# Expert outputs combined through a one-hot matrix in fp32r, with the expert rows in two parts, the routing weights as scalars of the sum, the last stores issued by ACT, and one more load buffer

## The chip, the cores and the metric

The kernel runs on one core of a Trainium2 chip. The metric is the device time of one execution in microseconds, as the median of three runs. A profile of one more execution gives the span of the engines' work and every instruction in it. The engines are named PE (TensorE, matmuls), PEld (its weight loads), DVE (VectorE), ACT (ScalarE), POOL (GpSimd) and SP (SyncE, which here only issues DMAs).

## What is computed

A layer has two sub-layers on 256 tokens of 2048 channels, in float32. The first is a mixer (three token mixers, gated and projected); the change leaves its arithmetic alone. The second is a mixture of 16 SwiGLU experts, of which each token uses two. Cut to that:

```
h = rms_norm(x, g_norm_ffn) * (1 + scale_f) + shift_f
affinity = sigmoid(h @ w_router)                      # 16 experts
e_idx = the two best experts of the best group of four, by affinity + b_router
w_sel = affinity[e_idx] / sum(affinity[e_idx])
combine = sum(one_hot(e_idx) * w_sel)                 # tokens x 16
for e in range(16):
    act = silu(h @ w_gate[e]) * (h @ w_up[e])         # 2048 -> 1024
    y += combine[:, e:e+1] * (act @ w_down[e])        # 1024 -> 2048
x = x + gate_f * y
```

## The kernel before

**Two stretches.** Until about 853 us the mixer runs; its weights arrive in fp32, ACT casts each to a high part and DVE subtracts for a low part (type fp32r, `split_w`, L168 and L169; `split_to`, L173 and L174, does the same for other tiles), and PE multiplies three products per pair (L331 to L333). A short router stretch follows. From 869.58 us to the end the experts run, one after the other.

**One expert.** Each expert has 64 slots. `rank` (tokens x experts) says in which slot of an expert a token sits, and `cmb` its weight. A one-hot matrix `O` (tokens x slots, bf16, L1007) gathers the expert's tokens: matmuls of `h2`, the normed activations in three bf16 parts, with `O` (L1075). `Or` (L1015) and the matmuls at L1063 give each slot its token's scale `rB` (copied by ACT, L1065); DVE makes `X` of it (L1079, L1081), the expert's input with channels on the partitions. The weights of the expert come in 24 loads of 1 MiB (`load_e`, L853, all issued by SP): 8 for gate, 8 for up, 8 for down. Each load feeds one unit of four fp32 matmuls of 64 rows into a tile `ring` of PSUM (L1110; a unit leaves 8 records in the trace, since an fp32 matmul leaves two). There are three `ring` tiles. After a gate or up sum ACT copies the ring to `graw` (L1132, one buffer), PE transposes it (L1137), and ACT's SiLU (L1145) or DVE's product (L1151) makes `sgt` and `A`. The down weights give the expert's rows in two halves of 1024 channels; DVE multiplies each by the gate vector `gfB` into a tile `y` (L1163).

**The combine before.** `scatter` makes `OT` (slots x tokens, fp32): DVE builds a one-hot that already holds the weights (L1094), PE transposes it (L1095), ACT copies it (L1097). `combine_part` multiplies `OT` with 512 columns of `y` in fp32 (L1170) and DVE adds the result to `x2` (L1171); eight such parts make an expert.

**Order.** `up_unit`, `gate_unit` of the next expert and `down_unit` follow each other, and after each unit `between` takes one small job from the lists `soon` (gather and scatter of the next expert) and `todo` (combine parts). A scheduler then sets the order on each engine from its own estimates, so what stands where is read from the program, below. Each engine works through its own row in order.

**Load buffers.** Loads rotate through a stock of 1 MiB buffers: 17 when the experts begin (named `wr`, `ws` and `m` after their pools: 11 `wr`, 3 of the pool of the split weights, 3 of the four `m`), 14 from expert 0's down unit on, when one pool is given back. The fourth `m` buffer is used for `y` (`m_tile`), which takes one of the `m` in turn.

**The end.** The last expert's down weights come as four column blocks of two loads each. `give_out` combines one block, and SP stores each 128x512 piece of the result (L1223). Behind it stands a loop for experts with more tokens than slots (L1238 on), which this input does not enter.

Of the kernel before, what the change touches and what calls it, by code (L numbers as in the profile page):

```python
# [20 lines left out]
P = 128  # L21
# [32 lines left out]
def kernel(  # L54
# [707 lines left out]
    mH, mL = [[m_tile([P, KD // 2, S], F32R) for _ in range(2)] for _ in range(2)]  # L762
# [47 lines left out]
    r2 = constb.tile([P, NT], F32, name="r2c")  # L810
    shT = constb.tile([P, KD], F32)
# [50 lines left out]
    for n in range(4):  # L862
# [7 lines left out]
        for k0 in range(0, KD, 4):  # L870
# [15 lines left out]
            if n == 3 and k0 == KD - 4:  # L886
                rotate([wraw] * NRAW + [wrawb] * NRAWB + [wrawc] * NRAWC + [wraw2] * NRAW2 + [wspl] * 3 +
                       [mt_pool] * (NM - 1))
# [5 lines left out]
        def h2_first(t):  # L894

            vc = fn.tile([P, 512], F32, name="tmp", bufs=3) if n < 3 else vc3[:, t, :]
# [9 lines left out]
        if n == 3:  # L906
            vc3, late_parts = m_tile([P, NT, 512], F32), []
        x2T = fn.tile([P, 4, S], F32, bufs=1)
        for t in range(NT):
            xc = x2[:, t, c0:c1]  # L910
            tmp = fn.tile([P, 512], F32, name="tmp", bufs=3)
# [7 lines left out]
            cp(x2T[:, :, t * P:(t + 1) * P], pst.rearrange("p (k s) -> p k s", s=P))  # L919
            for b in range(4):  # L920
                k = n * 4 + b
                pe.matmul(lgp[0:NE, t * P:(t + 1) * P], lhsT=wrA[:, k, :], rhs=x2T[:, b, t * P:(t + 1) * P],
# [21 lines left out]
    lgs = fn.tile([NE, S], F32, name="tmp", bufs=3)  # L944
# [60 lines left out]
    def one_hot(rke):  # L1005
        O = constb.tile([P, NT, CAP], BF16, name="O")
        dve.tensor_tensor(O, iota[:, 0:CAP].rearrange("p (o s) -> p o s", o=1).to_broadcast([P, NT, CAP]),  # L1007
                          rke.to_broadcast([P, NT, CAP]), op=ALU.is_equal)
        return O

# [48 lines left out]
    def gather(O, Or, X, kg=8):  # L1059

        ps = mx2()
        for t in range(NT):
            pe.matmul(ps[:, 0:CAP], lhsT=ones, rhs=Or[:, t, :], start=t == 0, stop=t == NT - 1)  # L1063
        rB = moe.tile([P, 1, CAP], F32, name="rB", bufs=1)
        act.copy(rB[:, 0, :], ps[:, 0:CAP])  # L1065
        for g in range(KD // kg):
            yield
            ps = mx2()
            for kk in range(kg):
# [3 lines left out]
                for t in range(NT):  # L1073
                    for part in h2:
                        pe.matmul(o, lhsT=part[:, t, k2 * 256 + j:(k2 + 1) * 256:2], rhs=O[:, t, :],  # L1075
                                  start=i == 0, stop=i == 5)
# [4 lines left out]
            dve.tensor_tensor(X[:, ks, :], X[:, ks, :],  # L1081
# [98 lines left out]
    def prepare(e, kg=8):  # L1180
# [6 lines left out]
        def weights():  # L1187
            state[e][1] = scatter(rke, cmb[:, :, e:e + 1])
# [94 lines left out]
```

## Time and profile before

| | us |
|---|---|
| median of three runs | 1869.71 |
| the three runs | 1869.63, 1869.71, 1872.86 |
| the profiled execution, its own time | 1873.41 |
| its span | 1871.7 |
| PE busy | 1770.6 (95%) |
| DVE busy | 884.0 (47%) |
| ACT busy | 426.2 (23%) |
| mean granted clock of PE | 0.99 |

The profile of the whole span mixes the two stretches. DVE and ACT have most of their work in the mixer; during the experts PE and the DMA engines carry nearly all. Busy shares over the whole span therefore say little; the rows below are from the stretch of the experts wherever it matters. "Idle before" in a row is the time the engine sat before that row, with the engine and instruction that ended it.

### The profile page before, as it was taken

Reading aid. Unit: us, or ns where it says so; the run is one execution under the profiler, and the core shown is the slowest. Engines: PE = TensorE matmul, PEld = TensorE weight load, DVE = VectorE, ACT = ScalarE, POOL = GpSimd, SP = SyncE. Lnnn points to the kernel's source line nnn. Section 1 sums busy time; section 2 is a strip of 40 time slices with the busy share of each in tenths; the row PEclk is TensorE's granted clock in tenths of the full one; section 3 lists DMA queues with packets and bytes.
Section 4 is the critical chain, followed back from the end, with each engine's and each line's share of the span. In section 5 each row is a group of like instructions: output and inputs, shape, how many; then the busy total and the mean of one; then the engine's idle time right before and its main releaser. Section 6 shows DMA issues by size and latency. Waiting matters only on the chain. (4 is left out here: it accounts for less than half of the span.)

```text
span 1871.7 us, 23342 instructions
## 1 busy us (share of the span) xinstructions
PE 1770.6 (95%) x9747; PEld 1061.2 (57%) x9748; DVE 884.0 (47%) x1116; ACT 426.2 (23%) x568; POOL 105.7 (6%) x100
## 2 busy tenths in 40 slices
PE   5999999999999999998999999999999999999996
PEld 4889789788788888774433333333343333333332
DVE  6769699978888895664121211221122112221211
ACT  2522346564444444452100000000000000000000
POOL 1000030300212201000000000000000000000000
PEclk9999999999999999998999999999999999999998
DMA  9998877659998996956999999999999999999993
GB/s 309 388 320 300 318 258 245 222 203 330 328 336 318 350 353 220 314 180 256 362 416 418 416 416 416 418 418 416 383 410 418 416 398 402 419 416 414 389 359 113
DMA packets 189230, 644.92 MB, mean 345 GB/s; under 512 B 17820, under 2 KB 26432, under 8 KB 155968
## 3 DMA queue, kind: packets, MB, share of 16 engines
q1 hardware_dynamic: 180720, 639.68, 88.9%
q0 software_dynamic: 2128, 3.38, 0.9%
q8 instruction: 78, 1.28, 0.3%
q10 hardware_dynamic: 6272, 0.32, 0.2%
q14 instruction: 32, 0.26, 0.0%
HBM read 641.18 MB, written 2.16 MB: 344 GB/s over the span
## 5 line engine op out<-in xcount | busy, mean ns | idle before, releaser
L169 DVE TENSOR_TENSOR ws<-wr,ws 128x1024 fp32r<-128x1024 f32 x226 | 293.5, 1304 | 106.9 <-ACT ws L168 105.6
L168 ACT CAST ws<-wr 128x1024 fp32r<-128x1024 f32 x226 | 236.5, 1049 | 303.5 <-PE dn L333 223.2
L1110 PE MATMUL ring<-wr,X 128*64 128x512 f32 x1224 | 281.5, 597 | 0.0
L332 PE MATMUL dn<-ws,hH 128*128 128x512 f32 x480 | 191.4, 399 | 0.8 <-DVE ws L169 0.8
L331 PE MATMUL dn<-ws,hH 128*128 128x512 f32 x480 | 191.1, 398 | 0.9 <-ACT ws L168 0.9
L333 PE MATMUL dn<-ws,hL 128*128 128x512 f32 x480 | 190.8, 398 | 0.0
L1132 ACT COPY graw<-ring 128x1024 f32<-128x1024 f32 x32 | 32.4, 1012 | 671.5 <-PE ring L1110 671.5
L1110 PEld LDWEIGHTS ring<-wr,X 128*64 128x64 f32 x1224 | 88.0, 137 | 170.4 <-issue 150.1
L289 DVE SCALAR_TENSOR_TENSOR acc_r<-wr,cs,acc_r 128x1024 f32<-128x1024 f32 x120 | 155.9, 1299 | 2.1 <-DMA wr<-in_w_ada_dram 1.1
L1171 DVE TENSOR_TENSOR x<-mx,x 128x512 f32<-128x512 f32 x128 | 88.5, 692 | 136.0 <-PE mx L1170 136.0
L1170 PE MATMUL mx<-m,OT 128*128 128x512 f32 x256 | 130.9, 621 | 9.2 <-DVE X L1079 3.7
L1110 PE MATMUL ring<-wr,A 128*64 128x512 f32 x552 | 132.3, 602 | 0.0
L1151 DVE TENSOR_TENSOR A<-mx,sgt 128x512 f32<-128x512 f32 x16 | 11.1, 692 | 249.6 <-PE mx L1137 249.6
L1137 PEld LDWEIGHTS mx<-id,graw 128*128 128x128 f32 x512 | 61.6, 191 | 82.8 <-ACT graw L1132 58.0
L331 PEld LDWEIGHTS dn<-ws,hH 128*128 128x128 f32 x480 | 90.9, 189 | 22.1 <-ACT ws L168 1.3
L332 PEld LDWEIGHTS dn<-ws,hH 128*128 128x128 f32 x480 | 91.1, 190 | 21.6 <-DVE ws L169 1.0
L333 PEld LDWEIGHTS dn<-ws,hL 128*128 128x128 f32 x480 | 91.0, 190 | 21.1
L1137 PE MATMUL mx<-id,graw 128*128 128x64 f32 x512 | 69.7, 281 | 32.9 <-ACT graw L1132 31.8
L1110 PE MATMUL ring<-ws,X 128*64 128x512 f32 x416 | 96.3, 596 | 0.0
L1163 DVE TENSOR_TENSOR m<-ring,gfB 128x1024 f32<-128x1024 f32 x30 | 36.7, 1225 | 121.2 <-PE ring L1110 121.2
L1110 PE MATMUL ring<-m,X 128*64 128x512 f32 x408 | 93.8, 595 | 0.0
L1015 DVE TENSOR_SCALAR Or<-iota,rank,r2c 128x64 f32<-128x64 f32 x32 | 8.7, 311 | 175.6 <-PE mx L1063 175.6
(409 smaller groups left out, 2335.7 us busy)
## 6 DMA issues: line engine op xcount, KB each, us to landing
wr<-in_w_in_dram SPq DMA_DIRECT2D x89, 1024.0 KB, 7.4
wr<-in_w_e_gate_dram SPq DMA_DIRECT2D x79, 1024.0 KB, 10.6
wr<-in_w_e_up_dram SPq DMA_DIRECT2D x74, 1024.0 KB, 14.4
wr<-in_w_e_down_dram SPq DMA_DIRECT2D x69, 1024.0 KB, 14.8
wr<-in_w_ada_dram SPq DMA_DIRECT2D x64, 1024.0 KB, 6.8
wr<-in_w_ada_dram SPq DMA_DIRECT2D x64, 512.0 KB, 8.6
m<-in_w_e_down_dram SPq DMA_DIRECT2D x30, 1024.0 KB, 12.1
ws<-in_w_e_down_dram SPq DMA_DIRECT2D x29, 1024.0 KB, 15.1
```

The costliest lines, as they stand in the source:

```text
L168: lately[0] = act.copy(h[:, 0:n], raw)
L169: lately[1] = dve.tensor_tensor(l[:, 0:n], raw, h[:, 0:n].bitcast(F32), op=ALU.subtract)
L289: dve.scalar_tensor_tensor(ac, wk, cs[:, k:k + 1], ac, op0=ALU.mult, op1=ALU.add)
L331: pe.matmul(o, lhsT=a, rhs=wH, start=first, stop=False)
L332: pe.matmul(o, lhsT=a, rhs=wL, start=False, stop=False)
L333: lately[2] = pe.matmul(o, lhsT=b, rhs=wH, start=False, stop=last)
L1110: pe.matmul(acc[j * CAP:(j + 1) * CAP, cc, :], lhsT=lhs[:, k + j, :], rhs=rhs[j], start=k == 0, stop=k == last)
L1132: act.copy(raw, acc.rearrange("p a b -> p (a b)"))
L1137: pe.matmul(ps[:, b * CAP:(b + 1) * CAP], lhsT=raw[:, b * P:(b + 1) * P], rhs=id2[:, 0:CAP], start=True, stop=True)
L1163: dve.tensor_tensor(y[:, cl], acc.rearrange("p a b -> p (a b)"), late[0][:, cl], op=ALU.mult)
L1170: pe.matmul(ps, lhsT=OT[:, t * P:(t + 1) * P], rhs=y[:, cl], start=True, stop=True)
L1171: dve.tensor_tensor(x2[:, t, cl], ps, x2[:, t, cl], op=ALU.add)
```

## The change

The one-hot matrix `O` gets 128 columns instead of 64 and serves twice: its first 64 columns for the gather as before, and all 128 for the scatter, where PE multiplies it with a bf16 identity (L1096 after). `OT` is then a plain one-hot of type fp32r. The weights enter later: DVE's sum multiplies by `cmb` as a scalar of each token (L1177). DVE's product with `gfB` writes each half of the expert's rows to `graw` (L1164), and `split_to` makes a high part (ACT, L173) and a low part (DVE, L174) of it in fp32r, in a pool of its own with two buffers. A combine part is then two fp32r matmuls (L1176). The gather's jobs are cut differently: the `rB` matmuls come after the first group of gather matmuls, so there is one job fewer.

The fourth `m` buffer, no longer needed for `y`, joins the stock of load buffers: 18 when the experts begin, 15 later. At the end ACT issues the stores. The last expert still combines in fp32 with the same `OT` read as fp32. Before the experts, some buffers of the router stretch are renamed or made smaller, and the second of two pieces of `h2` parts (`h2_rest`) is placed behind two router steps.

```diff
@@ stock of load buffers, set in the last block of w_out
-                rotate([wraw] * NRAW + ... + [wspl] * 3 + [mt_pool] * (NM - 1))
+                rotate([wraw] * NRAW + ... + [mt_pool] * 2 + [wspl] * 3 + [mt_pool] * 2)
@@ def one_hot(rke):
-        O = constb.tile([P, NT, CAP], BF16, name="O")
+        O = constb.tile([P, NT, 2 * CAP], BF16, name="O")
@@ def gather(O, Or, X, kg=8):
-        ps = mx2()
-        for t in range(NT):
-            pe.matmul(ps[:, 0:CAP], lhsT=ones, rhs=Or[:, t, :], start=t == 0, stop=t == NT - 1)
-        rB = moe.tile([P, 1, CAP], F32, name="rB", bufs=1)
-        act.copy(rB[:, 0, :], ps[:, 0:CAP])
         for g in range(KD // kg):
-            yield
             ps = mx2()
...
+            if g == 0:
+                pr = mx2()
+                for t in range(NT):
+                    pe.matmul(pr[:, 0:CAP], lhsT=ones, rhs=Or[:, t, :], start=t == 0, stop=t == NT - 1)
+                rB = moe.tile([P, 1, CAP], F32, name="rB", bufs=1)
+                act.copy(rB[:, 0, :], pr[:, 0:CAP])
...
+            yield
@@
-    def scatter(rke, cme):
+    def scatter(O):
         ps = mx2()
         for t in range(NT):
-            OC = moe.tile([P, P], F32, name="OC", bufs=1)
-            dve.tensor_scalar(OC, iota, rke[:, t, :], cme[:, t, :], op0=ALU.is_equal, op1=ALU.mult)
-            pe.transpose(ps[:, t * P:(t + 1) * P], OC, ident)
-        OT = moe.tile([P, S], F32, name="OT", bufs=3)
+            pe.matmul(ps[:, t * P:(t + 1) * P], lhsT=O[:, t, :], rhs=ident_b, start=True, stop=True)
+        OT = moe.tile([P, S], F32R, name="OT", bufs=3)
         act.copy(OT, ps[:, 0:S])
@@ def down_unit(wd, A):
-        y = m_tile([P, D], F32)
+        ys = []
         for hf in range(2):
             acc = unit(A, lambda k2: wd[:, k2, :, hf * 1024:(hf + 1) * 1024], 4)
-            dve.tensor_tensor(y[:, cl], acc.rearrange("p a b -> p (a b)"), late[0][:, cl], op=ALU.mult)
-        return y
+            y = moe.tile([P, 1024], F32, name="graw", bufs=1)
+            dve.tensor_tensor(y, acc.rearrange("p a b -> p (a b)"), late[0][:, hf * 1024:(hf + 1) * 1024],
+                              op=ALU.mult)
+            yp = late[1].tile([P, 2, 1024], F32R, name="y", bufs=2)
+            split_to(yp[:, 0, :], yp[:, 1, :], y)
+            ys.append(yp)
+        return ys
@@ def combine_part
-        pe.matmul(ps, lhsT=OT[:, t * P:(t + 1) * P], rhs=y[:, cl], start=True, stop=True)
-        dve.tensor_tensor(x2[:, t, cl], ps, x2[:, t, cl], op=ALU.add)
+        for i, y in enumerate(parts):
+            pe.matmul(ps, lhsT=OT[:, t * P:(t + 1) * P], rhs=y, start=i == 0, stop=i == len(parts) - 1)
+        dve.scalar_tensor_tensor(x2[:, t, cl], ps, cme[:, t, :], x2[:, t, cl], op0=ALU.mult, op1=ALU.add)
@@ the end
-    y_last = m_tile([P, D], F32)
+    OT, cme = OT.bitcast(F32), cmb[:, :, NE - 1:NE]
+    y_last = late[1].tile([P, D], F32, name="y", bufs=2)
...
-            sp.dma_start(out=out_v[:, t, cl], in_=x2[:, t, cl])
+            act.dma_start(out=out_v[:, t, cl], in_=x2[:, t, cl])
```

**PE, from the last gather matmul of a down phase to the next expert's up unit, one of the regular experts.** A name before `<-` is what is written; `ring` with `A` is a down unit (four matmuls), `ring` with `X` a unit of the gate or up that follows. Before:

```order
L1095 MATMUL mx<-ident,OC 128x128
L1110 MATMUL ring<-wr,A 64x512 x4
L1095 MATMUL mx<-ident,OC 128x128
L1170 MATMUL mx<-m,OT 128x512 x2
L1110 MATMUL ring<-wr,A 64x512 x4
L1170 MATMUL mx<-m,OT 128x512 x2
L1110 MATMUL ring<-wr,A 64x512 x4
L1110 MATMUL ring<-ws,A 64x512 x4
L1110 MATMUL ring<-ws,X 64x512 x8
```

After:

```order
L1096 MATMUL mx<-ident_b,O 128x128
L1111 MATMUL ring<-m,A 64x512 x4
L1176 MATMUL mx<-y,OT 128x512 x4
L1111 MATMUL ring<-m,A 64x512 x4
L1176 MATMUL mx<-y,OT 128x512 x4
L1111 MATMUL ring<-wr,A 64x512 x8
L1111 MATMUL ring<-wr,X 64x512 x4
L1176 MATMUL mx<-y,OT 128x512 x2
```

The two transposes that stood around a ring unit are two matmuls in a row; the first combine of half 0 stands one ring unit behind the first of them in both, now with four fp32r matmuls (high, high, low, low) where two fp32 ones stood, and the first combine of half 1 now comes one ring unit after that half is complete, where before it waited for the gate's transposes.

**DVE, in the same place of the program.** `m` or `graw` from `ring` is the product of a half, `y` the low part. Before:

```order
L1163 TENSOR_TENSOR m<-ring,gfB 128x1024
L1079 TENSOR_TENSOR X<-mx,rB 128x512
L1094 TENSOR_SCALAR OC<-iota,rank,cmb 128x128
L1081 TENSOR_TENSOR X<-X,shT 128x512
L1007 TENSOR_TENSOR O<-iota,rank 128x128
L1094 TENSOR_SCALAR OC<-iota,rank,cmb 128x128
L1171 TENSOR_TENSOR x_5591<-mx,x_5591 128x512 x4
L1163 TENSOR_TENSOR m<-ring,gfB 128x1024
L1151 TENSOR_TENSOR A<-mx,sgt 128x512
```

After:

```order
L1164 TENSOR_TENSOR graw<-ring,gfB 128x1024
L1081 TENSOR_TENSOR X<-mx,rB 128x512
L1009 TENSOR_TENSOR O<-iota,rank 128x256
L1083 TENSOR_TENSOR X<-X,shT 128x512
L174 TENSOR_TENSOR y<-graw,y 128x1024
L1177 SCALAR_TENSOR_TENSOR x_5591<-mx,cmb,x_5591 128x512 x4
L1164 TENSOR_TENSOR graw<-ring,gfB 128x1024
L174 TENSOR_TENSOR y<-graw,y 128x1024
L1177 SCALAR_TENSOR_TENSOR x_5591<-mx,cmb,x_5591 128x512
L1152 TENSOR_TENSOR A<-mx,sgt 128x512
```

The low part of half 0 stands behind the second product and shift of `X` and the one-hot; that of half 1 directly behind its product.

**SP, the last DMAs of the experts.** Before:

```order
L853 DMA wr<-in_w_e_down_dram 128x4x512 x2
L853 DMA m<-in_w_e_down_dram 128x4x512
L1223 DMA out_dram<-x_5591 128x512 x2
L853 DMA m<-in_w_e_down_dram 128x4x512 x2
L853 DMA wr<-in_w_e_down_dram 128x4x512
L1223 DMA out_dram<-x_5591 128x512 x6
```

After:

```order
L855 DMA m<-in_w_e_up_dram 128x2048 x2
L855 DMA ws<-in_w_e_up_dram 128x2048 x3
L855 DMA m<-in_w_e_down_dram 128x4x512 x2
L855 DMA wr<-in_w_e_down_dram 128x4x512 x6
L1249 COMPARE_AND_BRANCH
```

No store stands among the loads any more; the eight stores are the last DMAs in ACT's row, behind the last copy to `graw`.

## Rows read from the trace of the kernel before

**Rows 1.** Windows: stretch, length, busy time (instructions) by engine, granted clock, DMA share, GB/s
```profile
500.00:600.00 100.00, 100.00 (x436) 81.20 (x435) 86.85 (x73) 41.77 (x42) 19.33 (x11) 1.00 0.93 343
...
930.00:1812.00 882.00, 840.29 (x4858) 329.76 (x4856) 179.06 (x282) 43.46 (x70) 0.00 (x0) 1.00 1.01 410
1000.00:1300.00 300.00, 285.67 (x1597) 110.10 (x1595) 60.13 (x97) 15.48 (x25) 0.00 (x0) 1.00 1.02 417
```

**Rows 2.** Waits of PE, 930 to 1812 us: who for whom, us in total, times, longest
```profile
PE mx L1137 <- ACT graw L1132: 31.8, 27, 1.4
PE mx L1170 <- DVE X L1079: 3.7, 4, 1.0
PE mx L1075 <- ACT sgt L1145: 3.1, 13, 0.2
...
PE mx L1170 <- DVE m L1163: 1.3, 1, 1.3
```

**Rows 3.** Timeline of ACT: start, us, operation; the copies that end an up unit
```profile
1271.52 1.01 ACT L1132 COPY graw<-ring 128x1024 f32<-128x1024 f32 x1 [22.51 <-PE ring L1110]
...
1332.88 1.01 ACT L1132 COPY graw<-ring 128x1024 f32<-128x1024 f32 x1 [22.51 <-PE ring L1110]
...
1396.10 1.01 ACT L1132 COPY graw<-ring 128x1024 f32<-128x1024 f32 x1 [24.26 <-PE ring L1110]
...
1765.79 1.01 ACT L1132 COPY graw<-ring 128x1024 f32<-128x1024 f32 x1 [22.51 <-PE ring L1110]
...
1828.30 1.01 ACT L1132 COPY graw<-ring 128x1024 f32<-128x1024 f32 x1 [35.27 <-PE ring L1110]
```

**Rows 4.** Timeline of PE in the down phase of a regular expert
```profile
1248.28 0.33 PE L1095 MATMUL mx<-ident,OC 128*128 128x128 f32 x1
1248.44 1.88 PE L1170 MATMUL mx<-m,OT 128*128 128x512 f32 x4
1250.25 1.94 PE L1110 MATMUL ring<-wr,A 128*64 128x512 f32 x8
```

**Rows 5.** Groups of PE instructions, 930 to 1812 us: count, busy us, mean ns, idle before
```profile
L1170 PE MATMUL mx<-m,OT 128*128 128x512 f32 x232 | 118.5, 620 | 6.8 <-DVE X L1079 3.7 <-ACT OT L1097 1.8 <-DVE m L1163 1.3
...
L1075 PE MATMUL mx<-O,h 128*128 128x64 bf16 x1344 | 48.2, 193 | 3.1 <-ACT sgt L1145 3.1
```

**Rows 6.** Groups of the whole span (the page): the split of weights in the mixer
```profile
L169 DVE TENSOR_TENSOR ws<-wr,ws 128x1024 fp32r<-128x1024 f32 x226 | 293.5, 1304 | 106.9 <-ACT ws L168 105.6
L168 ACT CAST ws<-wr 128x1024 fp32r<-128x1024 f32 x226 | 236.5, 1049 | 303.5 <-PE dn L333 223.2
```

**Rows 7.** Timeline of DVE in the down phase of a regular expert
```profile
1245.61 1.23 DVE L1163 TENSOR_TENSOR m<-ring,gfB 128x1024 f32<-128x1024 f32 x1 [1.12 <-PE ring L1110]
1246.75 0.68 DVE L1079 TENSOR_TENSOR X<-mx,rB 128x512 f32<-128x512 f32 x1
...
1248.20 0.28 DVE L1007 TENSOR_TENSOR O<-iota,rank 128x128 bf16<-128x128 f32 x1
...
1249.50 0.69 DVE L1171 TENSOR_TENSOR x<-mx,x 128x512 f32<-128x512 f32 x1 [0.51 <-PE mx L1170]
1250.36 0.69 DVE L1171 TENSOR_TENSOR x<-mx,x 128x512 f32<-128x512 f32 x1 [0.17 <-PE mx L1170]
```

**Rows 8.** Timeline of SP's queue in the tail
```profile
1812.15 0.51 SPq L853 DMA_DIRECT2D m<-in_w_e_down_dram  x1
1838.55 1.22 SPq L1223 DMA_DIRECT2D out_dram<-x  x2
1839.81 1.07 SPq L853 DMA_DIRECT2D m<-in_w_e_down_dram  x2
```

**Rows 9.** Timeline of PE in the tail
```profile
1845.98 3.68 PE L1110 MATMUL ring<-m,A 128*64 128x512 f32 x8 [5.46 <-DMA m<-in_w_e_down_dram]
1850.45 1.12 PE L1170 MATMUL mx<-m,OT 128*128 128x512 f32 x2 [0.80 <-DVE m L1234]
```

**Rows 10.** Window of that unit, columns as in rows 1
```profile
1846.00:1850.00 4.00, 3.66 (x8) 0.74 (x8) 0.29 (x1) 0.00 (x0) 0.00 (x0) 0.50 1.03 386
```

More of the change, by code (lines that the diff above doesn't have):

```diff
@@ L760, in m_tile @@
         return t
-    mH, mL = [[m_tile([P, KD // 2, S], F32R) for _ in range(2)] for _ in range(2)]
+    mH, mL = zip(*[[m_tile([P, KD // 2, S], F32R) for _ in range(2)] for _ in range(2)])
     mgp, mg = open_pool(name="mgp", bufs=2, side="right")
@@ L894, in h2_first @@
         def h2_first(t):
[L896 removed]
+            vc = fn.tile([P, 512], F32, name="vc", bufs=2)
             dve.tensor_tensor(vc, x2[:, t, c0:c1], gch[:, 1, :], op=ALU.mult)
@@ L942, in small @@
         return t
-    lgs = fn.tile([NE, S], F32, name="tmp", bufs=3)
+    lgs = fn.tile([NE, S], F32, name="tmp", bufs=2)
     dve.tensor_copy(lgs, lgp[0:NE, 0:S])
@@ L1074, in gather @@
                     for part in h2:
-                        pe.matmul(o, lhsT=part[:, t, k2 * 256 + j:(k2 + 1) * 256:2], rhs=O[:, t, :],
+                        pe.matmul(o, lhsT=part[:, t, k2 * 256 + j:(k2 + 1) * 256:2], rhs=O[:, t, 0:CAP],
                                   start=i == 0, stop=i == 5)
                         i += 1
+            if g == 0:
[4 more added lines that the diff above has]
+                act.copy(rB[:, 0, :], pr[:, 0:CAP])
             ks = slice(g * kg, (g + 1) * kg)
@@ L1184, in prepare @@
         state[e] = [X, None]
-        parts = gather(one_hot(rke), slot_scale(rke), X, kg) if e else gather(O0, Or0, X, kg)
+        O, Or = (one_hot(rke), slot_scale(rke)) if e else (O0, Or0)
+        parts = gather(O, Or, X, kg)
         def weights():
-            state[e][1] = scatter(rke, cmb[:, :, e:e + 1])
-        return [lambda: next(parts, 0)] * (KD // kg + 1) + [weights]
+            state[e][1] = scatter(O)
+        return [lambda: next(parts, 0)] * (KD // kg) + [weights]
     jobs = prepare(0, 4)
-    for job in jobs[0:3]:
-        job()
-    for t in range(NT):
-        h2_rest(t, late_parts[t])
-    soon += [jobs[3], jobs[4], jobs[5]]
+    jobs[0]()
+    jobs[1]()
+    h2_rest(0, late_parts[0])
+    with tc.issue_after(slot_scale.last.ins), tc.issue_after(sigm.ins):
+        h2_rest(1, late_parts[1])
+    soon += jobs[2:]
     sg = gate_unit(wg_v[0], state[0][0])
@@ L1205 @@
             late.append(lt.tile([P, D], F32, name="gfB"))
+            late.append(lt)
             row_bcast(late[0], 3, 0, D)
@@ L1208 @@
         assert len(soon) == 1
-        combine(state[e][1], down_unit(wd_v[e], A))
+        combine(state[e][1], cmb[:, :, e:e + 1], down_unit(wd_v[e], A))
     A, OT = up_unit(wu_v[NE - 1], state[NE - 1][0], sg), state[NE - 1][1]
@@ L1246 @@
                 dve.tensor_scalar(rke, rke, -float(CAP), None, op0=ALU.add)
-                X, OT = x_tile(), scatter(rke, cme)
-                list(gather(one_hot(rke), slot_scale(rke), X))
+                O, X = one_hot(rke), x_tile()
+                OT = scatter(O)
+                list(gather(O, slot_scale(rke), X))
                 sg = gate_unit(wg_v[bass.ds(ev, 1)][0], X)
@@ L1252 @@
                 flush()
-                combine(OT, down_unit(wd_v[bass.ds(ev, 1)][0], A))
+                combine(OT, cme, down_unit(wd_v[bass.ds(ev, 1)][0], A))
                 flush()
```

36 lines of the change are left out of this document (19 added, 17 removed).

## The prediction

> **What bounds the kernel now.** I read the windows first. From 930 to 1812 us, the stage in which the experts follow each other without a gap, TensorE is busy 840.29 of 882 us at a granted clock of 1.00, while the DMA engines move 410 GB/s; in its best 300 us they move 417 GB/s at a share of 1.02 [rows 1]. So two resources are nearly full together. The view of waits tells which of them ends last: TensorE waits 31.8 us for ACT's copies of a finished gate or up sum, 3.7 us for X, 3.1 us for the SiLU, and in no row for a load [rows 2], so its own instructions and these small waits set the pace. ACT's copies at the end of each up unit give the beat: 1271.52, 1332.88, a period of 61.36 us; a long one to 1396.10, 63.22 us; the last from 1765.79 to 1828.30, 62.51 us [rows 3]. Of the 14 periods between the up units of expert 1 and 15, ten are regular to the hundredth, three like the long one (1.5 to 1.9 us over, together 4.9) and one is the last. The floor below that is the DMA: an expert has 24 loads of 1 MiB, 25.17 MB, at 417 GB/s 60.4 us. A regular expert thus has only 1.0 us to the floor, except that 14 to 17 loads of stock let TensorE run ahead of the DMA for a while.
>
> **The combine, per expert.** Eight fp32 matmuls of 128x512 stand as 16 records. From 930 to 1812 the group has 232 records, 118.5 us [rows 5], 14.5 experts at 8.2 us. The row at 1248.44 shows four records, 1.88 us, with the next ring unit starting 1.81 us after them [rows 4]; with that overlap in each of some five groups 7.7 us of path are left. Two such matmuls end 0.86 us apart, as the starts of the sums at 1249.50 and 1250.36 show [rows 7]: 8 x 0.86 = 6.9, so 0.8 us of the 7.7 is the filling of the groups. After, there are 16 fp32r matmuls (two parts by eight). Between 500 and 600 us, where fp32r matmuls of 128x512 keep TensorE full, 436 of them take 100.00 us [rows 1], 0.23 us each: 16 x 0.23 = 3.7 us, and with as many groups 0.9 us of filling: 4.6 us. **Saved 3.1 us.** The type is the same in both, so I see little room in this term.
>
> **The scatter.** Two fp32 transposes with a ring unit between them, the row at 1248.28 with 0.33 us, of which 0.16 us pass before the next starts [rows 4], so 0.3 to 0.6 us of path with the change of kind, become two bf16 matmuls of 128 columns in a row. The trace has 64-column bf16 matmuls, 1344 in 48.2 us [rows 5], 0.036 us each, so about 0.07; the fp32r row at 512 columns bounds it at 0.23. Saved 0.4 us (0 to 0.5). On DVE the two weighted one-hots (L1094) go and the bf16 one-hot doubles its columns, 0.28 us [rows 7] to at most 0.56. The SiLU wait, 3.1 us over 13 experts, goes with the new place of the gather: 0.2 us.
>
> **The split, which is new.** The half result of an expert was written by one DVE product (L1163, 1.23 us) and was read much later. Now that product goes to a buffer, ACT casts it to the high part (as L168 of the same shape, 1.05 us), and DVE subtracts for the low part (as L169, 1.30 us) [rows 6, 7]. Per expert that is 2 x 1.05 on ACT and 2 x 1.30 on DVE, engines idle most of the stage. What counts is that the order now puts the combine close behind. *Half 0:* the high part is ready 1.23 + 1.05 + 0.1 = 2.4 us after the ring's last matmul; TensorE has 12 gather matmuls, the scatter and one ring unit to do, 0.4 + 0.1 + 1.87 (the 1.94 us of a unit less that overlap of 0.07 [rows 4]) = 2.4 us: wait 0.1. The 0.1 for handovers is an estimate. On DVE the subtraction stands behind a second X product, the one-hot and the X shift: 1.14 + 0.68 + 0.28 + 0.68 + 1.30 = 4.1 us, and TensorE arrives after 2.5 + 0.46 (two high matmuls): wait 1.15. *Half 1:* one ring unit, 1.87 us, covers 2.4: wait 0.55; low part at 2.4 + 1.3 = 3.7 against 2.86: wait 0.85. With 0.15 for starting again **2.8 us are added** (both ends: 0 if the order hides it; 7.2 if neither half is covered at all). DVE's sums (L1177) keep their shape, 0.69 us [rows 7]; a scalar more costs at most a little, and nobody waits for them. I also name what queues behind: half 1's product waits for the one buffer `graw` until half 0 is split, 4.1 us against a half of 7 us; ACT's next `graw` copy comes 10 us later. Neither ends last.
>
> So a regular period is 61.36 - 3.1 - 0.4 - 0.2 + 2.8 = 60.5 us, right at the DMA's 60.4.
>
> **Long periods and the last one.** The long periods come where the order interleaves the combine of the expert before with the second transpose, with waits of up to 1 us for X, four in all the stage [rows 2, 3]; after the change all experts have one order, so 4.9 us goes. The last period has no expert to prepare, 12 combine matmuls instead of 8, and a wait of 1.3 us for the half; it saves 1.5 x 3.1 + 1.3 less about 2.5 of the new waits: 3.5 us.
>
> **The stores and the buffer.** In the tail SP issues a load at 1812.15 us; the next instruction in its row is a store of the output that needs DVE's sum, so it sits until 1838.55, and only then, at 1839.81, do the next loads follow, two at once, so that their buffers were free before [rows 8]. TensorE then waits 5.46 us for that load, and its next unit takes 3.68 us [rows 9] instead of the 1.94 of [rows 4], at a granted clock of 0.50, the lower level of 1.2 GHz [rows 10]. With the stores on ACT, which has nothing to do there, these loads leave some 20 us sooner: 5.5 + 1.7 us go. Against that the new order puts the wait for the last product (0.8 us each [rows 9]) into all four quarters, where before two of them ran beside a unit: 1.6 us. **Saved 5.5 us.** The last store is the same transfer from another queue: 0. The Trainium skill, DMA: Bandwidth & Descriptors, section "Issuing engines are not separate DMA queues", speaks against this gain: whoever starts a DMA, it runs on the same 16 engines, and starting it elsewhere saves only the time of issuing. By that the tail would save about 3 us of issue at most and the time would be some 2.5 us higher; the rows on SP show a wait in front of loads instead, and I go by them. The buffer in stock (17 to 18, later 14 to 15) is worth 0 where TensorE sets the pace, up to one load (2.5 us) where the DMA does.
>
> **The start.** Before the experts the change moves small pieces (half of the late h2 parts on DVE behind the slot scale, the rB matmuls behind the first gather group): between +0.7 and -1; the first one and a half experts then save their 0.9 each. I take -1.5 at the second up unit.
>
> **Rivals.** (a) *The waits are hidden and the DMA decides.* If the low parts come in time, TensorE would need 57.7 us per expert and eat its stock; the 882 us x 410 GB/s of [rows 1] at 417 take 867 us, so the loads now issued by 1812 land 15 us sooner and the last ones, without the pause, near 1812; from 1845.98 to the end of the span three loads' work took 25.7 us, so one load's work and the stores take 13 to 20: a span of 1829, about 1831 in all. For it: DVE and ACT are mostly idle. Against it: the DVE order with the subtraction fourth in line. (b) *The waits are larger*, since each handover between engines costs more than the 0.1 I give, or fp32r groups fill more slowly: a further 0.9 us per expert eats the combine's net gain, and long periods, last period and tail remain, 1869.7 - 14 = 1856. (c) *Slower: the clock.* Two new waits per expert, before the low parts, sit between short bursts. If each made the gate fall, the next unit would cost 1.74 us more [rows 4, 9]: 2 x 15 x 1.74 = 52 us, 1843 + 52 = 1895; it decides from some length of wait between 1.4 us, the longest in [rows 2], and 5.46 us. My new waits are below 1.2 us, so it takes waits several times longer than I work out. The Trainium skill, TensorE: Matmul & The Clock Gate, section "A second HAM failure mode: psum-queue depth-cycling", reports that frequent micro-idles between groups of matmuls can make the gate swing; here the waits for ACT's copies, 27 in 31.8 us [rows 2], leave the window at 1.00 [rows 1], so the trace does not bear that out at this size. (d) *Nothing moves*, because DMA and TensorE trade places and every saved microsecond turns into a wait for a load: excluded for the tail, and the floor lies 1.0 us under the period; about 1869.
>
> **How the numbers follow.** 13 periods x 0.9 = 11.7; long ones 4.9; last one 3.5; start 1.5; tail 5.5: 27.1 us. The profiled execution took 1873.41 us (span 1871.7), so its like would take 1846.3; it lies 3.7 us over the median 1869.71, and against that median I forecast 1842.6, said as **1843**. Chances: forecast 0.60 (1836 to 1850), (a) 0.17, (b) 0.15, (c) 0.05, (d) 0.03. The range for 8 in 10, 1832 to 1858, takes in (b) and nearly (a). About 0.2% is what a measurement of this kernel can tell from no change; faster 0.92, same 0.03, slower 0.05.
>
> **What would show it.** In the profile after: `graw` copies 60.5 us apart, all alike; TensorE's waits at the combine line for DVE near 30 us and for ACT near 10 over the stage, combine busy near 4 us an expert; DMA share near 1.02 throughout; no store in SP's row and no wait of TensorE over 2 us in the tail, the clock 1.00 there. Periods under 60 would mean (a), waits for loads in the stage the DMA's floor. Wrong altogether would be periods at or over 61.4 or a clock under 1.00 in the stage.

## The result, and the profile after

| | before | after |
|---|---|---|
| median, us | 1871.28 (four runs, 1869.63 to 1874.0) | 1853.03 (four runs, 1850.74 to 1854.29) |
| the profiled execution, us | 1873.41 | 1852.96 |
| its span | 1871.7 | 1851.2 |
| PE busy | 1770.6 | 1733.7 |

The ratio of the times is 0.990, with a 95% interval of 0.9882 to 0.9917: about 18 us faster. The forecast was 1843 us. It had the direction right, and the time lies inside its range of 1832 to 1858. It is 10 us over the forecast, though, and outside the narrower 1836 to 1850 that the prediction gave six chances in ten.

The two traces can be laid side by side at four places that both have: the last fp32r matmul of the mixer, the first ring unit of the experts, the up copies of expert 1 and 15, and the end. The first of these is in code whose arithmetic the change leaves alone; it only hands out the buffers `mH` and `mL` there in another order. Timeline of PE, the kernel before and then the changed one, last fp32r matmul of the mixer:

```profile
852.82 0.39 PE L333 MATMUL mx<-ws,m 128*128 128x512 f32 x1
```

```profile
847.59 0.39 PE L333 MATMUL mx<-ws,m 128*128 128x512 f32 x1
```

A part of these 5.2 us is chance: in the other profiles below the same matmul stands anywhere from 847.3 to 851.7 us, and at 849.8 in one whose program is that of the kernel before up to there. The execution in which the kernel before was profiled had the latest mixer of all. Another part may not be. The kernel before ran 25 times in all, beside this result and beside the experiments, with a mean of 1872.5 us. If what stands behind the mixer took as long each time as in the profile, its mixers end at 851.9 us on the mean. The same estimate from the 16 runs of the changed kernel and of three variants of it (`pin_combine`, `both_later` and `pin_all`, below) gives 848.7. Why the mixer should end some 3 us earlier after the change, no run shows. What follows is therefore measured from place to place.

| stretch | before | after | forecast of the difference | measured |
|---|---|---|---|---|
| mixer end to first ring unit | 16.76 | 17.10 | } -1.5 | +0.3 |
| first ring unit to up copy of expert 1 | 93.29 | 89.62 | } | -3.7 |
| 14 periods to the up copy of expert 15 | 865.43 | 858.37 | -20.1 | **-7.1** |
| from there to the end of the span | 43.40 | 38.52 | -5.5 | -4.9 |

Together these stretches save 15.3 us. What is missing against the forecast sits in the 14 periods. ACT's up copies of the changed kernel, to be set against [rows 3] (start, us, operation):

```profile
1016.62 1.01 ACT L1133 COPY graw<-ring 128x1024 f32<-128x1024 f32 x1 [15.73 <-PE ring L1111]
...
1077.25 1.01 ACT L1133 COPY graw<-ring 128x1024 f32<-128x1024 f32 x1 [14.03 <-PE ring L1111]
...
1139.58 1.01 ACT L1133 COPY graw<-ring 128x1024 f32<-128x1024 f32 x1 [15.73 <-PE ring L1111]
...
1754.22 1.01 ACT L1133 COPY graw<-ring 128x1024 f32<-128x1024 f32 x1 [15.73 <-PE ring L1111]
...
1812.68 1.01 ACT L1133 COPY graw<-ring 128x1024 f32<-128x1024 f32 x1 [15.55 <-PE ring L1111]
```

A period of 60.63 us, near the 60.5 of the forecast, is followed by one of 62.33, and so on in turn through the whole stage: seven of the 13 periods before the last carry 1.5 to 1.7 us more. Where that time goes shows in PE's timeline at the second half's combine, first in a short period, then in a long one (idle before a row in brackets):

```profile
1063.28 0.50 PE L1176 MATMUL mx<-y,OT 128*128 128x512 f32 x1 [0.69 <-ACT y L173]
1064.54 0.50 PE L1176 MATMUL mx<-y,OT 128*128 128x512 f32 x1 [0.76 <-DVE y L174]
1064.97 8.80 PE L1111 MATMUL ring<-wr,X 128*64 128x512 f32 x40
...
1123.91 0.50 PE L1176 MATMUL mx<-y,OT 128*128 128x512 f32 x1 [0.69 <-ACT y L173]
1125.17 0.50 PE L1176 MATMUL mx<-y,OT 128*128 128x512 f32 x1 [0.76 <-DVE y L174]
1125.60 3.30 PE L1111 MATMUL ring<-ws,X 128*64 128x512 f32 x8
1128.68 3.98 PE L1111 MATMUL ring<-m,X 128*64 128x512 f32 x16
```

The waits are the same to the hundredth. After the second pair the first unit takes 3.30 us instead of the 1.94 of [rows 4], and the next two take 3.98. The windows say why (last three columns: granted clock, DMA share, GB/s):

```profile
1064.00:1072.00 8.00, 7.46 (x35) 2.65 (x37) 1.23 (x2) 0.00 (x0) 0.00 (x0) 1.00 1.01 421
...
1125.00:1129.00 4.00, 3.83 (x11) 1.36 (x13) 0.86 (x2) 0.00 (x0) 0.00 (x0) 0.63 1.01 418
1128.00:1132.00 4.00, 4.00 (x18) 1.18 (x16) 0.00 (x0) 0.00 (x0) 0.00 (x0) 0.82 1.01 420
1132.00:1136.00 4.00, 4.00 (x22) 1.36 (x20) 0.00 (x0) 0.00 (x0) 0.00 (x0) 1.00 1.00 413
```

Behind the second pair TensorE's clock falls to its lower level, 1.2 instead of 2.4 GHz (means of 0.63 and 0.82 in the windows from 1125 and from 1128 us), and it is back at 1.00 from 1132 us. The view of waits from 930 to 1800 us (who for whom, total, times, longest) has the rest; compare [rows 2]:

```profile
PE mx L1138 <- ACT graw L1133: 30.8, 27, 1.2
PE mx L1176 <- DVE y L174: 21.9, 28, 0.9
PE mx L1176 <- ACT y L173: 10.3, 15, 0.7
```

The waits for X, for the SiLU and for the half are gone; 32.2 us for the split halves have come. No wait for a load appears. In the tail, where [rows 9] showed 5.46 us for a load, PE now reads

```profile
1813.74 2.09 PE L1138 MATMUL mx<-id,graw 128*128 128x64 f32 x16 [1.11 <-ACT graw L1133]
1816.61 6.48 PE L1111 MATMUL ring<-m,A 128*64 128x512 f32 x16 [0.78 <-DVE A L1152]
```

and SP's queue, against [rows 8], ends early with nothing but loads:

```profile
1783.78 17.23 SPq L855 DMA_DIRECT2D wr<-in_w_e_down_dram  x6
```

So the wait for a load is gone, but the 16 records of two units take 6.48 us. In the kernel before the same two units read

```profile
1832.22 3.65 PE L1110 MATMUL ring<-ws,A 128*64 128x512 f32 x16 [0.85 <-DVE A L1151]
```

and in the changed kernel the windows from 1810 to 1820 and from 1820 to 1830 us show the clock at 0.78 and 0.88. That is 2.8 us more of the same kind.

### The profile page after: what moved, and what is told of

Same layout as the page of the kernel before. It is cut to its first block, busy times and chain, and to the rows that moved or that the text cites. A ratio compares the mean times of both kernels' runs of the same rounds, so it can differ in the third digit from the quotient of the medians.

```text
span 1851.2 us, 23367 instructions
## 1 busy us (share of the span) xinstructions
PE 1733.7 (94%) x9747; PEld 1050.2 (57%) x9748; DVE 914.2 (49%) x1114; ACT 459.0 (25%) x598; POOL 107.5 (6%) x101
## 4 chain that ended last, share of the span: by engine, by line
PE 82%; DVE 9%; issue 3%; ACT 3%; DMA 2%; SPq 1%; POOL 0%; ACTq 0%; DVEq 0%; POOLq 0%
PE ring L1111 35%; PE dn L331 8%; PE dn L332 8%; PE dn L333 8%; PE mx L1176 4%; PE mx L1138 4%; PE dn L370 3%; PE mx L1071 2%; DVE graw L1164 2%; DVE y L174 2%; ACT graw L1133 2%; PE dn L366 1%; DMA wr<-in_w_ada_dram 1%; PE dn L342 1%; PE dn L343 1%
## 5 line engine op out<-in xcount | busy, mean ns | idle before, releaser
L1111 PE MATMUL ring<-wr,X 128*64 128x512 f32 x1096 | 253.8, 608 | 0.0
L1111 PEld LDWEIGHTS ring<-wr,X 128*64 128x64 f32 x1096 | 76.2, 139 | 146.0 <-issue 142.5
L1111 PE MATMUL ring<-wr,A 128*64 128x512 f32 x576 | 137.2, 603 | 0.0
L1177 DVE SCALAR_TENSOR_TENSOR x<-mx,cmb,x 128x512 f32<-128x512 f32 x128 | 92.0, 746 | 85.1 <-PE mx L1176 85.0
L1111 PE MATMUL ring<-m,X 128*64 128x512 f32 x544 | 129.0, 609 | 0.0
L1176 PE MATMUL mx<-y,OT 128*128 128x512 f32 x256 | 92.3, 452 | 35.5 <-DVE y L174 21.9
L1176 PEld LDWEIGHTS mx<-y,OT 128*128 128x128 f32 x256 | 41.4, 188 | 108.5 <-ACT y L173 34.6
L1164 DVE TENSOR_TENSOR graw<-ring,gfB 128x1024 f32<-128x1024 f32 x30 | 36.7, 1224 | 121.9 <-PE ring L1111 101.8
```

What stands on the lines that cost most here:

```text
L1111: pe.matmul(acc[j * CAP:(j + 1) * CAP, cc, :], lhsT=lhs[:, k + j, :], rhs=rhs[j], start=k == 0, stop=k == last)
L1164: dve.tensor_tensor(y, acc.rearrange("p a b -> p (a b)"), late[0][:, hf * 1024:(hf + 1) * 1024], op=ALU.mult)
L1176: pe.matmul(ps, lhsT=OT[:, t * P:(t + 1) * P], rhs=y, start=i == 0, stop=i == len(parts) - 1)
L1177: dve.scalar_tensor_tensor(x2[:, t, cl], ps, cme[:, t, :], x2[:, t, cl], op0=ALU.mult, op1=ALU.add)
```

## The experiments

**The stores alone.** The kernel before, with one line changed.

```diff
-            sp.dma_start(out=out_v[:, t, cl], in_=x2[:, t, cl])
+            act.dma_start(out=out_v[:, t, cl], in_=x2[:, t, cl])
```

> The kernel before, with its last stores issued by ACT and nothing else changed. Theory (a store in SP's row held the last three loads): no wait of TensorE for a load in the tail, no unit of 3.68 us there, the time from the last up copy to the end of the span 43.4 - 5.5 - 1.7 = 36.2 us, time 6 to 7 us under the kernel before. Rival (the queue that issues makes no difference beyond the time of issuing): at most 3 us of the 43.4 go.

Measured: 1861.54 us (four runs, 1860.82 to 1863.22) against 1872.06 for the kernel before, ratio 0.9944 (0.9925 to 0.9962), so 10.5 us. From the last up copy to the end 33.7 us instead of 43.4. SP's queue and PE in the tail of this kernel:

```profile
1809.28 9.43 SPq L853 DMA_DIRECT2D m<-in_w_e_down_dram  x3
1818.75 0.51 SPq L853 DMA_DIRECT2D wr<-in_w_e_down_dram  x1
```

```profile
1835.70 5.37 PE L1110 MATMUL ring<-m,A 128*64 128x512 f32 x24
```

The last load leaves at 1818.75 instead of 1840.93, and three units run in one piece where PE sat 5.46 us. The tail is 9.7 us shorter, more than the 7.2 us expected. The order that the scheduler finds without stores among the loads has more units side by side, so one of the three waits for the last product (0.8 us each) went too. A further 1.1 us lies between the last combine and the end (8.0 us instead of 9.0); no run shows why. The Trainium skill, DMA: Bandwidth & Descriptors, section "Issuing engines are not separate DMA queues", says that another issuing engine saves only the time of issuing. That is not all that the move saves here: this run shows a gain of 10 us, because SP issues in its own order and a store that waits held back the loads behind it.

**The stores back on SP, in the changed kernel.**

> The changed kernel with its last stores issued by SP again. In SP's row four of the last eight loads now stand behind stores, not behind the first. Theory (a store in front of a load delays it until DVE's sum is there): the load of the fourth block leaves after a store, near 1833 us, and lands up to 3 us late; from the last up copy to the end 38.5 + 0 to 4 us. Rival (the order with the new combine keeps loads in front, so the move to ACT is worth nothing in this kernel): 38.5 within 0.5 us.

Measured: 1851.77 us in one run, and 39.2 us from the last up copy to the end. Three of the four loads behind a store do arrive late:

```profile
1831.85 1.94 PE L1111 MATMUL ring<-wr,A 128*64 128x512 f32 x8 [0.73 <-DMA wr<-in_w_e_down_dram]
...
1837.58 1.94 PE L1111 MATMUL ring<-wr,A 128*64 128x512 f32 x8 [1.02 <-DMA wr<-in_w_e_down_dram]
1840.12 1.94 PE L1111 MATMUL ring<-wr,A 128*64 128x512 f32 x8 [0.60 <-DMA wr<-in_w_e_down_dram]
```

Together 2.35 us, where the kernel with stores on ACT has none. The tail is only 0.7 us longer than the 38.5 us of the changed kernel, since the clock's fall in it costs less: its two units take 5.10 us, not 6.48. Without the fall the tail would be 2 us longer. So the move is worth 10 us in the old order and, by one profile, about 2 in the new one, whose scheduler places only half of the last eight loads behind stores. This kernel also tells something else: its combine is that of the changed kernel, its waits too (22.0 and 10.4 us), but the clock falls in the fifth period and then in every second one, five times, not seven. Two falls fewer are 3.4 us, so its time says nothing against the stores on ACT.

**Which wait lets the clock fall.** Two kernels take waits out by moving combine parts, not by removing what they wait for: `pin_half1` the pair of the second half, `half0_later` the wait of the first. `pair.mm` is the last matmul of the latest ring unit in program order; `unit.mms[1]` that of the second unit of the second half.

```diff
# pin_half1: parts of the second half behind the unit that calls for them
+        with tc.issue_after(pair.mm.ins) if n // 2 == 1 and len(parts) > 1 else nullcontext():
             for i, y in enumerate(parts):
                 pe.matmul(ps, lhsT=OT[:, t * P:(t + 1) * P], rhs=y, ...)
# half0_later: parts of the first half one unit later
+                after = unit.mms[1] if n < 2 else None
+        with tc.issue_after(after.ins) if after else nullcontext():
```

> Only the parts of an expert's second half are pinned behind later units; the first half's combine stays where it was, with its 0.87 us wait for the low part. Theory (the pair of waits at the second half, 0.69 and 0.76 us around a burst of 0.43 us, is what lets the clock fall): no fall, all periods alike at 60.63 - 1.45 + 0.3 = 59.5 us. Rival (any wait of 0.8 us or more at the combine does it): the fall stays in every second expert, periods of 59.5 and 61.2 in turn.

> Only the first half's combine is moved, by one load unit; the second half keeps its two waits of 0.69 and 0.76 us. Theory (the pair at the second half lets the clock fall): the fall stays in every second expert, periods of 60.63 - 0.87 = 59.8 and 61.5 in turn. Rival (the first half's wait of 0.87 us, 11 us earlier, is needed for it): no fall, all periods 59.8 us.

Measured, `pin_half1`: 1825.99 us in one run. ACT's up copies:

```profile
1013.73 1.01 ACT L1133 COPY graw<-ring 128x1024 f32<-128x1024 f32 x1 [11.43 <-PE ring L1111]
...
1072.41 1.01 ACT L1133 COPY graw<-ring 128x1024 f32<-128x1024 f32 x1 [11.43 <-PE ring L1111]
...
1131.08 1.01 ACT L1133 COPY graw<-ring 128x1024 f32<-128x1024 f32 x1 [11.43 <-PE ring L1111]
...
1424.54 1.01 ACT L1133 COPY graw<-ring 128x1024 f32<-128x1024 f32 x1 [11.50 <-PE ring L1111]
...
1485.85 1.01 ACT L1133 COPY graw<-ring 128x1024 f32<-128x1024 f32 x1 [13.22 <-PE ring L1111]
```

Periods of 58.68 us, all alike, up to 1424.54. The first half's wait is still there (11.5 us in 14 times), and the clock reads 1.00 over the stage, in which the changed kernel had seven falls; every stretch of 4 us between 930 and 1780 us reads 1.00:

```profile
1051.32 0.74 PE L1177 MATMUL mx<-y,OT 128*128 128x512 f32 x2 [0.86 <-DVE y L174]
```

```profile
930.00:1800.00 870.00, 825.20 (x4933) 324.54 (x4930) 216.13 (x291) 76.29 (x101) 0.00 (x0) 1.00 1.02 416
```

The period is 0.8 us better than expected, partly because a combine part now covers some of the wait for ACT's copy at the up unit (0.46 us instead of 1.11). From 1424.54 on the periods are 60.2 to 61.3, with small waits for loads. In `half0_later`, 1841.96 us in one run, it is the other way round:

```profile
1061.89 0.49 PE L1180 MATMUL mx<-y,OT 128*128 128x512 f32 x1 [0.69 <-ACT y L173]
1063.15 0.49 PE L1180 MATMUL mx<-y,OT 128*128 128x512 f32 x1 [0.77 <-DVE y L174]
```

The pair is there, and periods of 60.1 and 61.8 us mix, as in these up copies:

```profile
1015.76 1.01 ACT L1136 COPY graw<-ring 128x1024 f32<-128x1024 f32 x1 [14.02 <-PE ring L1111]
...
1075.86 1.01 ACT L1136 COPY graw<-ring 128x1024 f32<-128x1024 f32 x1 [14.02 <-PE ring L1111]
...
1137.66 1.01 ACT L1136 COPY graw<-ring 128x1024 f32<-128x1024 f32 x1 [15.72 <-PE ring L1111]
```

Five of the 14 carry 1.7 us more, at no regular distance. So in the stage the first half's wait is not needed for a fall, and the second half's pair is. Whether it takes two waits, or only as much idle time close together as their 1.45 us, no run separates: the longest single wait of the stage before is 1.4 us [rows 2].

**One wait of the pair.** The low parts are left out of the combine; they are still made.

```diff
+        parts = parts[:1]
         for i, y in enumerate(parts):
```

> The changed kernel with the low parts left out of the combine (they are still made): one fp32r matmul per part instead of two. At the second half the wait of 0.69 us for the high part stays, the 0.76 us for the low part behind it goes, and so does the first half's 0.87 us. Theory (it takes the two waits close together to let the clock fall): no fall, first periods 60.63 - 0.87 - 0.76 - 8 x 0.23 = 57.2 us, then the DMA's 60.4. Rival (the wait of 0.69 us at that place is enough): periods with 1.7 us more among the first.

Measured: 1829.23 us in one run. The 0.69 us for the high part stay, alone:

```profile
1058.71 0.50 PE L1177 MATMUL mx<-y,OT 128*128 128x512 f32 x1 [0.69 <-ACT y L173]
1059.14 8.80 PE L1111 MATMUL ring<-wr,X 128*64 128x512 f32 x40
```

Four periods of 56.5 to 56.8 us without a fall, then 60.2 to 61.4 with waits for loads. The four alone would decide nothing, since `sp_stores`, with the pair, also has its first four without a fall. But the wait comes 15 times in the stage, and every stretch of 4 us between 930 and 1780 us reads 1.00:

```profile
PE mx L1177 <- ACT y L173: 9.8, 15, 0.7
```

```profile
930.00:1800.00 870.00, 797.33 (x4818) 305.36 (x4814) 211.55 (x291) 77.22 (x101) 0.00 (x0) 1.00 1.02 416
```

That one wait of 0.69 us at that place is not enough is likely, then, and not shown strictly: from about the fifth expert on waits for loads change the pattern. The 27 waits of 1.17 us for ACT's copies bring no fall in the stage of any kernel; the pair, with a burst of 0.50 us between its two waits, does in about every second or third case.

**All parts moved away.** Either every part is pinned behind the unit that calls for it (`pin_combine`), or the first half by one unit and the second half as in `pin_half1` (`both_later`).

> Each combine part is pinned behind the load unit after which the code asks for it, so the parts of an expert stand in the next expert's up and gate units, far behind the split. Theory (in the changed kernel the short waits for the split halves, 0.87 + 0.69 + 0.76 us per expert, both cost their own length and let TensorE's clock fall in every second expert, 1.7 us each time): no wait of TensorE at the combine line, every period between up copies alike, 60.63 - 2.3 + 0.6 for three more groups = 58.9 us, granted clock 1.00 in the whole stage, the last up copy near 1779 us, time near 1819 us (1812 to 1830). Rival A (the clock falls for another reason, such as the change between kinds of matmul): periods still alternate by 1.7 us. Rival B (the DMA decides as soon as TensorE needs less): waits of TensorE for loads, periods not under 60.4, time near 1840.

> The first half's combine is moved by one load unit, the second half's parts are pinned behind later units; nothing else differs from the changed kernel. Theory (waits at the split, and the clock falls that the second half's pair brings, are all that the order costs): no waits for the split halves, granted clock 1.00, first periods 58.68 - 0.87 + 0.1 = 57.9 us, then the DMA's 60.4; time 1823 to 1829. Rival (the first half's place matters to the clock too): periods with 1.7 us more among them.

Measured: 1828.3 us (1826.75 to 1832.32), ratio to the kernel before 0.9766 (0.9744 to 0.9789), and 1828.38 us (1827.25 to 1832.28), ratio 0.977 (0.9747 to 0.9793). No wait for a split half, no fall of the clock in the stage, and first periods of 58.21 and 58.15 us. Both then change to 60.2 to 61.4 us, after six such periods, with waits for loads. In the tail the clock does fall in both, as in the changed kernel: the two units behind the last up copy take 5.35 us instead of 3.65. Of `pin_combine` I had expected 1819 us: I took it that a stock of 15 loads, 38 us of DMA, lets TensorE run ahead to the end. It lasts for six periods that run 2.2 us or more ahead of the DMA and one of 1 us: some 15 us, six loads.

**TensorE relieved further.** In `pin_all` all small jobs are pinned, the transposes after ACT's copies too.

```diff
         for jobs in (soon, todo):
             if jobs:
+                with tc.issue_after(pair.mm.ins):
                     return jobs.pop(0)()
```

> All small jobs are pinned behind the load unit that calls for them: combine parts, gather and scatter, and the transposes that follow ACT's copy, so that the copy (1.17 us of wait, twice per expert) is covered by a unit. Theory (once the waits at the split are gone the DMA decides after some eight experts, as in the run with combine parts pinned alone, 58.2 us first and 60.2 to 61.4 later): first periods near 58.2 - 2.2 = 56.0 us, then from about the fourth or fifth expert on 60.4 with waits for loads; the last load lands at the same time, so the time stays within 4 us of 1828. Rival (TensorE still decides): 14 x 2.2 us less than with combine parts pinned alone, near 1800.

Measured: 1828.12 us (1826.89 to 1831.24), ratio 0.9759 (0.9739 to 0.9779). In the stage the 1.17 us waits for ACT's copy are gone, and the first periods are 56.04 us; then (up copies, and waits of PE from 930 to 1800 us):

```profile
1070.59 1.01 ACT L1134 COPY graw<-ring 128x1024 f32<-128x1024 f32 x1 [11.62 <-PE ring L1112]
...
1126.63 1.01 ACT L1134 COPY graw<-ring 128x1024 f32<-128x1024 f32 x1 [11.63 <-PE ring L1112]
...
1186.00 1.02 ACT L1134 COPY graw<-ring 128x1024 f32<-128x1024 f32 x1 [11.62 <-PE ring L1112]
...
1246.39 1.01 ACT L1134 COPY graw<-ring 128x1024 f32<-128x1024 f32 x1 [11.63 <-PE ring L1112]
```

```profile
PE ring L1112 <- DMA wr<-in_w_e_down_dram: 16.4, 28, 0.6
PE ring L1112 <- DMA m<-in_w_e_down_dram: 6.8, 11, 0.6
```

The fourth period is 59.37, the fifth 60.39 us. The lead of about 14 us is spent after three experts instead of six, and the time is the same to 0.3 us: from there on the DMA sets the pace. The nine periods from the fifth on take 60.8 us on the mean, 0.4 more than the 60.4 worked out from [rows 1]. These waits for loads, the longest of them 0.94 us, do not make the clock fall in the stage; in the tail it falls here too (5.35 us for the two units).

**Without the split.** The changed kernel with one fp32 part and an fp32 one-hot: eight fp32 matmuls per expert, as before the change.

```diff
-        OT = moe.tile([P, S], F32R, name="OT", bufs=3)
+        OT = moe.tile([P, S], F32, name="OT", bufs=3)
...
-            y = moe.tile([P, 1024], F32, name="graw", bufs=1)
+            y = late[1].tile([P, 1024], F32, name="y", bufs=2)
...
-            split_to(yp[:, 0, :], yp[:, 1, :], y)
-            ys.append(yp)
+            ys.append(y)
...
```

> The changed kernel, with the expert rows left whole in fp32 and the one-hot matrix in fp32: the combine is eight fp32 matmuls again, and the weights stay scalars of the sum. Theory (the split brings 3.1 us per expert less matmul, and pays 2.3 us of waits plus 0.85 us of clock on average): no wait of TensorE for a split half, clock 1.00, all periods alike at 61.36 - 0.6 = 60.8 us, so the stage takes as long as with the split, within 0.5 us a period. Rival (the split is a net gain as placed): periods at 61.3 or more on average.

Measured: 1845.1 us in one run. Up copies:

```profile
1077.10 1.01 ACT L1133 COPY graw<-ring 128x1024 f32<-128x1024 f32 x1 [25.78 <-PE ring L1111]
...
1137.99 1.01 ACT L1133 COPY graw<-ring 128x1024 f32<-128x1024 f32 x1 [25.78 <-PE ring L1111]
```

Periods of 60.89 us, all alike but the first, one of 61.17 and the last; the clock at 1.00, no waits at the combine. The 14 periods take 850.8 us against 858.4 in the changed kernel, 0.54 less in each. From the first gate copy, 881.7 us here and 881.6 there, to the end it is 8 us shorter: where the changed kernel puts them, the two fp32r parts cost more than the eight fp32 matmuls that they replace. The clock makes the difference: where it holds, the changed kernel's period of 60.63 is 0.26 us under these 60.89.

**The buffer.** One load buffer fewer (17 and later 14), in the changed kernel and in `both_later`.

```diff
-                       [mt_pool] * 2 + [wspl] * 3 + [mt_pool] * 2)
+                       [mt_pool] * 2 + [wspl] * 3 + [mt_pool])
```

> The changed kernel with one load buffer fewer, 17 and later 14 as before the change. Theory (TensorE sets the pace in the changed kernel, so a buffer more buys nothing): the periods stay 60.63 us where the clock holds and 62.3 where it falls, no waits for loads, from the first gate copy to the last up copy within 2 us of 931 (the falls do not come at the same experts in each execution, 1.7 us each). Rival (the buffer is worth a load): 2.5 us more.

> The kernel in which both halves' combine parts stand later, with one load buffer fewer. Theory (there the DMA decides from about the eighth expert on, and a buffer is one load of lead taken before the router's pause): the periods of 58.15 us end about one expert sooner, the time is 0 to 2.5 us over the 1828.4 of the same kernel with the buffer. Rival (the buffer matters only where loads are late by chance): no difference in where the first long period comes.

Measured, `stock17`: 1849.48 us in one run, periods of 60.6 and 62.3 us in turn, no waits for loads; from the first gate copy to the last up copy 929.4 us against 931.1 with the buffer, with six falls of the clock instead of seven. The buffer is worth nothing there. In `both17` the first longer period is the sixth (60.14 us), in `both_later` the seventh (59.64): one load of lead is gone. The time, 1830.08 us (1826.86 to 1832.82), is 1.7 us over, which its spread does not separate from none.

## Why the prediction was right, and where it was off

**What bounds the kernel.** Right. TensorE set the pace before and after, with the DMA close behind; `pin_all`, `pin_combine` and `both_later` show the DMA taking over as soon as TensorE needs less, with periods of 60.8 us on the mean where I had 60.4. Rival (a) gave 1831 us for a kernel whose waits are hidden; these three, in which they are hidden, took 1828.1 to 1828.4.

**The combine.** Forecast 4.6 us per expert, measured by the starts of the rows 5.2: the waits break the five groups into seven. Saved 2.5 instead of 3.1 us. (The 7.7 us of the kernel before should by their own terms be 7.8: 8.2 less five overlaps of 0.07.)

**The waits at the split.** Forecast 0.1, 1.15, 0.55 and 0.85 us, 2.8 with the restart; measured 0, 0.86, 0.69 and 0.76, 2.3 us. Both halves were found at the right place and in the right size from the order on DVE and durations of other lines of the trace.

**The regular period.** Forecast 60.5 us, measured 60.63 where the clock holds. That it is so close is in part luck: the combine saved 0.6 us less than forecast and the waits cost 0.5 less. The long periods of the kernel before are gone, as forecast (nine of its regular periods are alike to the hundredth, the tenth is 0.3 us longer). The last one takes 58.46 us, 4.05 less (forecast 3.5).

**The step that failed: the clock.** Rival (c) had the mechanism, half of the place (waits "before the low parts" that "sit between short bursts") and the price: 1.74 us each forecast, 1.70 measured in the stage. The wait before the low part of the first half, which it also counts, is not needed for a fall. I set it aside since each new wait is below 1.2 us and the trace before shows longer ones without a fall; I wrote that it takes "waits several times longer than I work out". That weighed the waits one by one. The runs show that in the stage a pair, 0.69 and 0.76 us around one short burst, does it where a single wait of 1.17 or of 0.86 us does not, and one of 0.69 did not. It fell in seven of the 14 periods, not at each of 30 waits: 11.7 us, and 2.8 us more in the tail. Without these 14.5 us the changed kernel would by estimate have been at 1838 to 1839, inside the 1836 to 1850 of the forecast. The Trainium skill, TensorE: Matmul & The Clock Gate, section "A second HAM failure mode: psum-queue depth-cycling", tells of one kernel, in bf16, in which TensorE idles briefly between groups of matmuls so often that the gate swings between its two levels. I had let one row of the trace before overrule it; the trace of the changed kernel agrees in kind, with its seven falls in the stage.

The prediction named its own signs of being wrong altogether: periods at or over 61.4, or a clock under 1.00 in the stage. Both came, with seven periods of 62.1 to 62.3 us and a window at 0.63. The time fell inside the range all the same, and some of that is luck. Of the times that the prediction names, 1856 for rival (b) is the nearest to the measured 1853, but (b)'s cause, larger waits, is not what happened: they were 2.3 us, not 2.8. The range was drawn to take in (b) and so took in the falls of the clock.

**The tail.** The mechanism, loads behind a store, is shown by the run with the stores alone, and it was mis-sized: 10.5 us in the old order instead of 5.5 to 7.2. In the changed kernel the term of 5.5 came out as 4.9: 7.7 saved, less 2.8 for the clock again.

**The start.** Forecast -1.5, measured -3.4 us (+0.3 and -3.7). Of the difference 1.1 us are two waits in the first combine of the kernel before, 0.64 us for X and 0.46 us for the one-hot near 938 us, which the trace after does not have and which I had left out.

**The buffer.** Forecast 0 where TensorE decides, up to one load where the DMA does: as measured.

**The sum.** Against the profiled execution I forecast 1846.3, and 1852.96 was measured. The clock added 14.5. The mixer took off 5.2, the start 1.9, the tail without the clock 2.2; the 13 periods without the clock added 1.9 (14.7 saved, 16.6 forecast) and the last took off 0.5: +6.6 of the +6.7.

**What stays open.** Why the clock falls at every second pair in the changed kernel, only from the fifth on in `sp_stores` and irregularly in `half0_later`, with waits equal to the hundredth, isn't shown by any run. Nor is why it falls in the tail of the changed kernel after waits of 1.11 and 0.78 us, while the kernel before and the one without the split have 1.17 and 0.85 us at that place and keep it. The size of the waits does not decide there: `hi_only` keeps the clock after waits as in the changed kernel,

```profile
1792.86 2.00 PE L1138 MATMUL mx<-id,graw 128*128 128x64 f32 x16 [1.11 <-ACT graw L1133]
1795.64 3.65 PE L1111 MATMUL ring<-m,A 128*64 128x512 f32 x16 [0.79 <-DVE A L1152]
```

and `pin_combine`, `both_later` and `pin_all` lose it after only 0.44 to 0.45 and 0.78 to 0.79 us, which `pin_half1` and `both17` have too and keep it.

## What to carry to other kernels

A split into two parts of a faster type moves work to other engines and puts a chain of handovers in front of the matmul. Before counting the cheaper matmuls, look at how many units of other work the order leaves between the product and its use; here moving it by one unit for one half and by several for the other (`both_later`) was worth 25 us. When new waits of TensorE are priced, price those that stand close together as one, with the clock in it; here such a pair cost 1.45 us of waiting and, at seven of 14 places, 1.70 us of clock. And look for stores among the loads in the row of the engine that issues both: here one that waited stood in front of three loads for 26 us.

## What the hardware showed that I had not expected

A fall of TensorE's clock does not need a long wait. 0.69 and 0.76 us with 0.50 us of matmuls between them brought 1.7 us of slow matmuls in five to seven of 14 cases (four kernels), while single waits of 1.17 us, 27 times in the stage, brought none. In the tail, after 16 short matmuls, even 0.44 and 0.78 us were followed by a fall in three kernels of five. And a stock of 15 loads is a lead of only some 14 to 16 us, six loads of 2.5 us: three kernels with first periods of 56.04, 58.15 and 58.68 us ran ahead for three, six and eight periods before they waited for the DMA.
